# A mixture-of-experts product: gelu half a block later, all splits on VectorE, pairs at another rate, and the scatters of the gate matrix in pairs behind marks

## The chip, the cores and the metric

The kernel runs on one core of one Trainium2 chip. The metric is the device time of the whole program in microseconds (us).

## The reference, cut to what matters

Two transformer blocks are computed for 256 tokens with D = 2048. The change lies in the last part of the second block, a mixture of 16384 experts of which each of 8 heads takes 16 per token:

```python
def peer_ffn(h, w_pq, sub_keys_1, sub_keys_2, w_u, w_v):
    q = (hf @ w_pq).reshape(T, PEER_HEADS, 2, PEER_HALF)
    s1 = jnp.einsum('thd,kd->thk', q[:, :, 0], sub_keys_1).astype(jnp.float32)
    s2 = jnp.einsum('thd,kd->thk', q[:, :, 1], sub_keys_2).astype(jnp.float32)
    v1, i1 = lax.top_k(s1, PEER_TOPK)
    v2, i2 = lax.top_k(s2, PEER_TOPK)
...
    sc, ci = lax.top_k(cand, PEER_TOPK)
...
    experts = e1 * PEER_KEYS + e2
    gates = jax.nn.softmax(sc, axis=-1).astype(h.dtype)
...
        u = jnp.take(w_u, ib, axis=0)
        a = jnp.einsum('td,tkd->tk', hb, u)
        c = gb * jax.nn.gelu(a)
        vv = jnp.take(w_v, ib, axis=0)
        return jnp.einsum('tk,tkd->td', c, vv)
```

## The kernel before, in words

The kernel does not gather rows of w_u per token. It computes the product of all 256 tokens with all 16384 experts, applies gelu, and multiplies by a matrix C that holds each token's gate at its experts and zero elsewhere. C has 128 partitions (the first key, e1) and 128 slices of 257 columns (the second key, e2; 256 tokens and one column of row numbers).

**The u product.** `u_block(e2)` runs for e2 = 0 to 127, in two half blocks b (i = 2 * e2 + b counts half blocks, 0 to 255). A half block has a 512 KB load of w_u into a tile wr (SP's queue, 4 buffers), its rounding to wh on ScalarE (`split_next`, line 1464, 2 buffers), the rest wl = wr - wh on VectorE or POOL (`low`, line 1469, 2 buffers) and 16 matmuls on TensorE (8 of 512 columns and 8 of 256, line 187, into the PSUM tile pp). `split_next(i + 1)` is written ahead of half block i's matmuls. At the end of an e2, line 1502 copies half of pp on ScalarE, 1503 adds the other half on VectorE and 1504 multiplies by a row on POOL (VectorE once all pairs are through). The gelu of that e2 (`tail`, lines 1481 and 1483 on ScalarE) and the product with C (line 1484, POOL, later VectorE) come in the next e2.

**What lies between.** `between` puts other work into each half block, in three phases. First the search for the top 16 (`topk_steps`, lines 1350 to 1420, most of it VectorE's), so many steps per half block as a budget of 18 allows, and then `finish`. In this phase `low` of every second half block is POOL's (line 1466), but for every eighth e2. Then the 128 pairs of tokens, one per half block: `pair_ops` builds one-hot rows (lines 1516 to 1521, VectorE and ScalarE), `pair_mms` multiplies them a half block later into a PSUM tile pq, and after two pairs `quad_end` brings four columns of gates into C (line 1537). Last `places`, which numbers the rows of C that are used by the tokens' first or second half.

**The scatters.** When the places are there, `send(e2)` writes slice e2 of C, 128 rows of 1088 bytes, to rows of a DRAM tensor cd, at the places `posi` (line 1584, an indirect DMA that POOL issues; 124 of them). `u_block`'s loop writes up to 6 of them behind each e2. The order of TensorE, ScalarE and VectorE is as written (`manual_schedule`); POOL's order is left to the scheduler. Behind the u product comes the v product: four slices of C with w_v loaded plainly, then 103 times a load of 128 rows of cd by SP (`fetch`, line 1712), a gather of rows of w_v by POOL (line 1714), their split (lines 1676 and 1683) and the matmuls into py.

Each engine works through its own order and waits at an instruction for semaphores that other engines or DMAs set.

Of the kernel before, what the change touches and what calls it, by code (L numbers as in the profile page):

```python
# [1282 lines left out]
def peer(nc, tc, io, xd, hT, rbc, hp, sp, W, ident, mm, raw_block, split_block, proj_T, blocks, power_rstd, new_pair):  # L1283
    cd = io["cd"]
    with ExitStack() as es:
# [35 lines left out]
        with ExitStack() as pu_stack:  # L1321
# [135 lines left out]
            def split_next(i):  # L1457

                e2, b = divmod(i, 2)
                if e2 == 128:  # L1460
                    return lambda: None
                raw = raw_block(io["w_u"][e2, b])
                hi = W["pool"].tile([128, 1024], F32R, name="wh", bufs=W["hi"])
                nc.scalar.activation(hi, raw, AF.Copy)  # L1464
                eng = nc.gpsimd if b and not topk_done and e2 % 8 else nc.vector

                def low():
                    lo = W["pool"].tile([128, 1024], F32R, name="wl", bufs=W["lo"])
                    eng.tensor_tensor(lo, raw, hi.bitcast(F32), op=OP.subtract)  # L1469
                    parts[i] = hi, lo  # L1470

                return low
# [14 lines left out]
            def u_block(e2):  # L1487
                P = pu.tile([128, 512], F32, name="pp")
                for b in range(2):
                    low = split_next(2 * e2 + b + 1)  # L1490
                    if b == 0:
                        tail()
                    between(low)
                    hi, lo = parts.pop(2 * e2 + b)
                    for j in range(8):
                        k = 8 * b + j
                        mm(P, hi[:, j * 128:(j + 1) * 128], hT[k].rearrange("p s t -> p (s t)"), k == 0, False)
                    for j in range(8):
                        k = 8 * b + j
                        mm(P[:, :256], lo[:, j * 128:(j + 1) * 128], hT[k][:, 0, :], False, k == KT - 1)  # L1500
# [24 lines left out]
            def pair_mms(p, ws):  # L1525
                if p % 2 == 0:
                    bank4[0] = pq.tile([128, 4, 128], F32, name="pq")
                for i, w in enumerate(ws):
                    t = 2 * p + i
                    for a in range(3):  # L1530
                        mm(bank4[0][:, t % 4, :], w[:, 0, :], w[:, 1 + a, :], t % 4 == 0 and a == 0, t % 4 == 3 and a == 2)
                    mm(cnt[:, t // 128, :], w[:, 0, :], w[:, 4, :], t == 0, t == 255)

            def quad_end(q4, n):
                t4 = slice(4 * q4, 4 * q4 + 4)
                v = bank4[0].rearrange("p t e -> p e t")
# [41 lines left out]
            sent = [0]  # L1578

            def send(e2):  # L1580


                src = C.rearrange("p a b -> p (a b)")[:, e2 * 257:e2 * 257 + CROW]
                i = nc.gpsimd.indirect_dma_start(cd, bass.IndirectOffsetOnAxis(posi[:, e2:e2 + 1], 0), src, None).ins  # L1584
# [8 lines left out]
            placing = None  # L1593

            def between(low):


                nonlocal pair, q4, left, topk_done, placing
                if not topk_done or fins:
# [7 lines left out]
                    left += 18  # L1607
# [5 lines left out]
                full = None  # L1613
                if waiting:
                    p, ws = waiting.pop()
                    pair_mms(p, ws)
                    if p % 2:
                        full = p // 2
                if pair < 128:
                    waiting.append((pair, pair_ops(pair)))  # L1620
                    pair += 1
                low()
                if placing and next(placing, "end") == "end":
                    placing = False
                if full is not None:
                    quad_end(full, done[0])
# [5 lines left out]
            pu_stack.enter_context(tc.manual_schedule(engines={mybir.EngineType.PE, mybir.EngineType.Activation, mybir.EngineType.DVE}))  # L1632
            split_next(0)()
            for e2 in range(128):
                u_block(e2)
                if placing is False:
                    for _ in range(6):
                        if sent[0] < min(e2 - 1, NC):
                            send(sent[0])
# [251 lines left out]
```

## Time and profile before

| | |
|---|---|
| median of 3 runs (lowest to highest) | 2949.1 us (2947.26 to 2950.67) |
| the profiled execution's own time | 2950.48 us |
| its span | 2948.7 us |
| mean granted TensorE clock | 0.971 |
| busy: PE, DVE, ACT, POOL | 94%, 64%, 54%, 27% |
| DMA, mean over the span | 191 GB/s |

Times in the profile are us from the span's start. PE is TensorE's matmuls, PEld its loads of weights, DVE is VectorE, ACT ScalarE, POOL GpSimd; SPq is the queue of DMAs that SP issues. L1464 is line 1464 of the kernel before. In a row of the timeline the bracket tells how long the engine was idle before the instruction and what ended that. "issue" means that the profile shows nothing it waited for, "remote" that a semaphore's setter is not shown.

### The profile page before, as it was taken

The page shows a single profiled execution, that of the slowest core. Times are in us where ns is not written, and L with a number is a line of the kernel's source. Part 1 is how long each engine was busy: PE and PEld are TensorE (multiplying, and loading weights), DVE is VectorE, ACT ScalarE, POOL GpSimd, SP SyncE. Part 2 cuts the span into 40 slices and gives each one's busy share as a digit, 9 for nine tenths or more (in the row PEclk, how much of TensorE's full clock was granted, in tenths as well). Part 3 has the DMA queues.
Part 4 walks back from the last instruction along what each step waited for, and adds up shares of the span by engine and source line. Part 5 has one row for each costly group of instructions (what it writes and reads, how often), then busy time and mean ns, then how long its engine had stood idle before and what let it go on. Part 6 is the DMA issues. An engine that isn't in the chain of part 4 may idle for free. (4 is left out here: it accounts for less than half of the span.)

```text
span 2948.7 us, 41341 instructions
## 1 busy us (share of the span) xinstructions
PE 2768.1 (94%) x14566; PEld 2301.3 (78%) x14566; DVE 1898.4 (64%) x3498; ACT 1588.6 (54%) x2951; POOL 798.5 (27%) x703
## 2 busy tenths in 40 slices
PE   8999999999999999999999899999994199999998
PEld 5867788887888888878887678888883087888886
DVE  7545576556766555565657878888882065766665
ACT  4445565445665544444544348888871054655554
POOL 6312320012310000111014442333337622322231
PEclk9999999999999999999999999999997599999999
DMA  6565443654446655666554344444445266988883
GB/s 224 177 223 189 134 139 123 218 187 154 147 144 208 209 183 167 215 211 193 183 179 157 134 157 158 159 158 161 160 144 189 98 216 236 359 298 285 299 308 133
DMA packets 158810, 561.74 MB, mean 191 GB/s; under 512 B 19584, under 2 KB 33536, under 8 KB 145024
## 3 DMA queue, kind: packets, MB, share of 16 engines
q1 hardware_dynamic: 137808, 433.71, 44.9%
q0 software_dynamic: 20784, 125.29, 11.4%
q8 instruction: 117, 1.92, 0.3%
q14 instruction: 101, 0.83, 0.1%
HBM read 531.17 MB, written 27.75 MB: 190 GB/s over the span
## 5 line engine op out<-in xcount | busy, mean ns | idle before, releaser
L204 DVE TENSOR_TENSOR wl<-wr,wh 128x1024 fp32r<-128x1024 f32 (+1 forms) x467 | 600.2, 1287 | 458.9 <-ACT wh L202 385.3
L187 PE MATMUL pp<-hT,wh 128*128 128x512 f32 x2880 | 754.4, 404 | 104.2 <-ACT wh L1464 53.3
L202 ACT ACTIVATE wh<-wr 128x1024 fp32r<-128x1024 f32 (+1 forms) x467 | 492.9, 1056 | 585.0 <-PE pp L187 495.5
L187 PE MATMUL pp<-wh,hT 128*128 128x512 f32 x2688 | 695.6, 399 | 4.6 <-ACT wh L202 2.7
L187 PEld LDWEIGHTS pp<-hT,wh 128*128 128x128 f32 x2880 | 525.0, 192 | 207.3 <-ACT wh L1464 58.8
L187 PEld LDWEIGHTS pp<-wh,hT 128*128 128x128 f32 x2688 | 501.3, 190 | 127.7 <-ACT wh L202 7.8
L187 PEld LDWEIGHTS pp<-hT,wl 128*128 128x128 f32 x2880 | 396.6, 192 | 57.8 <-issue 21.1
L187 PE MATMUL pp<-hT,wl 128*128 128x256 f32 x2880 | 406.6, 284 | 26.2 <-issue 20.3
L187 PE MATMUL pp<-wl,hT 128*128 128x512 f32 x1344 | 374.5, 400 | 12.1 <-DVE wl L204 12.1
L1469 DVE TENSOR_TENSOR wl<-wr,wh 128x1024 fp32r<-128x1024 f32 x230 | 278.7, 1221 | 116.3 <-issue 64.3
L187 PEld LDWEIGHTS pp<-wl,hT 128*128 128x128 f32 x1344 | 248.9, 190 | 70.6 <-DVE wl L204 15.4
L1464 ACT ACTIVATE wh<-wr 128x1024 fp32r<-128x1024 f32 x256 | 268.9, 1050 | 42.1 <-remote 33.1
L1676 ACT ACTIVATE hT<-vb 128x1024 fp32r<-128x1024 f32 x202 | 210.7, 1059 | 131.0 <-PE py L187 100.6
L1683 DVE TENSOR_TENSOR wr<-vb,hT 128x1024 fp32r<-128x1024 f32 x135 | 165.3, 1229 | 76.1 <-PE py L187 55.0
L1714 POOL DMA_INDIRECT vb<-w_v,cb x103 | 128.9, 1252 | 284.1 <-ACT hT L1676 99.7
L1584 POOL DMA_INDIRECT cd<-C,posi x124 | 137.6, 1110 | 138.0 <-DVE C L1484 89.5
L1521 ACT ACTIVATE oh<-oh,gP 128x128 bf16<-128x128 bf16 x512 | 162.0, 389 | 0.0
L187 PE MATMUL py<-hT,c 128*128 128x512 f32 x600 | 152.6, 389 | 0.0
L187 PE MATMUL py<-hT 128*128 128x512 f32 x592 | 150.4, 389 | 0.0
L187 PEld LDWEIGHTS py<-hT,c 128*128 128x128 f32 x600 | 112.6, 188 | 23.4
L187 PEld LDWEIGHTS py<-hT 128*128 128x128 f32 x592 | 111.1, 188 | 23.1
L1683 DVE TENSOR_TENSOR wl<-vb,hT 128x1024 fp32r<-128x1024 f32 x67 | 82.2, 1227 | 34.2 <-PE py L187 27.7
(445 smaller groups left out, 3162.4 us busy)
## 6 DMA issues: line engine op xcount, KB each, us to landing
wr<-w_u SPq DMA_DIRECT2D x256, 512.0 KB
wr<-w_even SPq DMA_DIRECT2D x104, 512.0 KB
wr<-w_out SPq DMA_DIRECT2D x96, 512.0 KB
wr<-w_odd SPq DMA_DIRECT2D x96, 512.0 KB
wr<-w_in SPq DMA_DIRECT2D x64, 512.0 KB
wr<-w_mem SPq DMA_DIRECT2D x32, 512.0 KB
wr<-w_pq SPq DMA_DIRECT2D x32, 512.0 KB
cb<-cd SPq DMA_DIRECT2D x103, 136.0 KB
```

The lines of the kernel that those rows point to most:

```text
L187: nc.tensor.matmul(out, lhsT=lhsT, rhs=rhs, start=start, stop=stop, skip_group_check=True)
L202: nc.scalar.activation(hi, raw, AF.Copy)
L204: (lo_eng or nc.vector).tensor_tensor(lo, raw, hi.bitcast(F32), op=OP.subtract)
L1464: nc.scalar.activation(hi, raw, AF.Copy)
L1469: eng.tensor_tensor(lo, raw, hi.bitcast(F32), op=OP.subtract)
L1521: nc.scalar.activation(w[:, 1 + a, :], w[:, 4, :], AF.Copy, scale=gP[:, a, t:t + 1])
L1584: i = nc.gpsimd.indirect_dma_start(cd, bass.IndirectOffsetOnAxis(posi[:, e2:e2 + 1], 0), src, None).ins
L1676: nc.scalar.activation(hi, src, AF.Copy)
L1683: nc.vector.tensor_tensor(lo, src, hi.bitcast(F32), op=OP.subtract)
L1714: nc.gpsimd.indirect_dma_start(v, None, wide, bass.IndirectOffsetOnAxis(c[:, 256:257].bitcast(I32), 0))
```

## The change

Line numbers shift by a few: 1469, 1484 and 1502 to 1504 are one lower in the changed kernel, and line 1584 is 1586.

- All of `low` is on VectorE.
- `tail` runs in the second half block of an e2 instead of the first, behind the rounding of the next half block.
- The budget for the top-k steps is 14 per half block instead of 18. The last step stands behind half block 76 instead of 59, and the first pair in half block 83 instead of 66.
- The pairs are spread so that they end in half block 194, as before: 94 half blocks have one, 17 have two.
- From half block 197 on, VectorE sets one element of the tile eT behind its `low` (line 1630), and two scatters follow on POOL, each behind a copy of that element (line 1585). 118 of the 124 scatters are sent so, and 6 behind the last `tail`. POOL's order is as written too.

```diff
-                eng = nc.gpsimd if b and not topk_done and e2 % 8 else nc.vector
...
-                    eng.tensor_tensor(lo, raw, hi.bitcast(F32), op=OP.subtract)
+                    nc.vector.tensor_tensor(lo, raw, hi.bitcast(F32), op=OP.subtract)
...
-                    if b == 0:
+                    if b:
                         tail()
-                    between(low)
+                    between(2 * e2 + b, low)
...
+                p = paced[0]
+                nc.gpsimd.tensor_copy(eT[:1, 1, e2:e2 + 1], eT[:1, 0, p:p + 1])
                 i = nc.gpsimd.indirect_dma_start(cd, bass.IndirectOffsetOnAxis(posi[:, e2:e2 + 1], 0), src, None).ins
...
+            q_end = 2 * 97
...
-                    left += 18
+                    left += 14
...
-                if waiting:
-                    p, ws = waiting.pop()
-                    pair_mms(p, ws)
+                full, ws = [], list(waiting)
+                waiting.clear()
+                if pair < 128 and q_from is None:
+                    q_from = i
+                for p, w in ws:
+                    b4 = pair_mms(p, w)
                     if p % 2:
-                        full = p // 2
-                if pair < 128:
+                        full.append((p // 2, b4))
+                while pair < 128 and pair * (q_end - q_from) < 128 * (i + 1 - q_from):
                     waiting.append((pair, pair_ops(pair)))
                     pair += 1
                 low()
+                if placing is False and sent[0] < NC:
+
+                    nc.vector.memset(eT[:1, 0, i:i + 1], 1.0)
+                    paced[0] = i
+                    for _ in range(2):
+                        if sent[0] < min(i // 2 - 1, NC):
+                            send(sent[0])
...
-            pu_stack.enter_context(tc.manual_schedule(engines={mybir.EngineType.PE, mybir.EngineType.Activation, mybir.EngineType.DVE}))
+            pu_stack.enter_context(tc.manual_schedule(engines={mybir.EngineType.PE, mybir.EngineType.Activation, mybir.EngineType.DVE,
+                                                             mybir.EngineType.Pool}))
...
-                if placing is False:
-                    for _ in range(6):
-                        if sent[0] < min(e2 - 1, NC):
-                            send(sent[0])
```

Three places show how the order moves. The first is ScalarE in the top-k phase, two half blocks before the change (junk and rbc are the two buffers that hold an e2's sums):

```order
L1502 ACTIVATE junk<-pp 128x256 [waits PE_49]
L1464 ACTIVATE wh<-wr 128x1024 [waits DMAHW4_49,Activation_49]
L1481 ACTIVATE C<-junk 128x256 [waits Pool_49]
L1464 ACTIVATE wh<-wr 128x1024 [waits DMAHW5_49,DVE_49,PE_49]
L1502 ACTIVATE rbc<-pp 128x256 [waits PE_49]
```

And the same place with the change:

```order
L1501 ACTIVATE rbc<-pp 128x256 [waits PE_49,Activation_49]
L1464 ACTIVATE wh<-wr 128x1024 [waits DMAHW6_49,DVE_49]
L1464 ACTIVATE wh<-wr 128x1024 [waits DMAHW7_49,DVE_49,PE_49]
L1480 ACTIVATE C<-rbc 128x256 [waits Pool_49]
L1501 ACTIVATE junk<-pp 128x256 [waits PE_49,Activation_49]
```

The gelu, which waits for POOL, stood between the two roundings of the weights, and now stands behind both.

The second place is VectorE in the same phase, before (L1350 to L1355 are steps of the top-k, pp is the product):

```order
L1503 TENSOR_TENSOR junk<-junk,pp 128x256 [waits Activation_49]
L1354 MAX C<-C 128x8 [waits DVE_49]
L1355 MAX_INDEX C<-C 128x8 [waits DVE_49]
L1350 MAX C<-C 128x8
L1351 MAX_INDEX C<-C 128x8 [waits DVE_49]
L1352 MATCH_REPLACE C<-C 128x128
L1469 TENSOR_TENSOR wl<-wr,wh 128x1024 [waits DMAHW5_49,PE_49,Activation_49]
```

With the change:

```order
L1502 TENSOR_TENSOR junk<-junk,pp 128x256 [waits Activation_49]
L1468 TENSOR_TENSOR wl<-wr,wh 128x1024 [waits DMAHW4_49,Activation_49]
L1350 MAX C<-C 128x8
L1351 MAX_INDEX C<-C 128x8 [waits DVE_49]
L1352 MATCH_REPLACE C<-C 128x128
L1354 MAX C<-C 128x8 [waits DVE_49]
L1355 MAX_INDEX C<-C 128x8 [waits DVE_49]
L1468 TENSOR_TENSOR wl<-wr,wh 128x1024 [waits DMAHW5_49,PE_49,Activation_49]
```

Every half block's wl is now in VectorE's order, with fewer steps of the top-k between two of them.

The third place is POOL at the first scatters, before:

```order
L1504 TENSOR_TENSOR rbc<-rbc 128x256 [waits DVE_49]
L1484 TENSOR_TENSOR C<-C,rbc 128x252 [waits Activation_49,Pool_49]
L1584 DMA cd<-C,posi 15872x272 [waits DVE_49]
L1584 DMA cd<-C,posi 15872x272 x7
L1584 DMA cd<-C,posi 15872x272 [waits DMASW0_49]
```

With the change:

```order
L1483 TENSOR_TENSOR C<-C,junk 128x252 [waits Activation_49,Pool_49]
L1503 TENSOR_TENSOR rbc<-rbc 128x256 [waits DVE_49]
L1585 COPY eT<-eT 1x1 [waits DVE_49]
L1586 DMA cd<-C,posi 15872x272
L1585 COPY eT<-eT 1x1
L1586 DMA cd<-C,posi 15872x272
L1585 COPY eT<-eT 1x1 [waits DVE_49]
```

Before, a scatter waits for the DMA eight ahead of it at most; now every second one also stands behind a copy that waits for VectorE.

## Rows read from the trace of the kernel before

**Rows 1.** Busy time of each engine, windows from the product's start to the end.

```profile
core 0: us, PE busy (x) PEld busy (x) DVE busy (x) ACT busy (x) POOL busy (x), PEclk, DMA share, GB/s
1536.00:1769.00 233.00, 205.99 (x1119) 176.30 (x1118) 183.01 (x551) 97.35 (x147) 104.82 (x91) 0.96 0.45 149
1769.00:2195.00 426.00, 425.85 (x3075) 376.76 (x3073) 375.18 (x1026) 353.03 (x894) 144.18 (x126) 1.00 0.47 158
...
2210.00:2233.00 23.00, 23.00 (x135) 20.31 (x135) 14.49 (x23) 11.25 (x16) 17.98 (x16) 1.00 0.88 286
2233.00:2363.00 130.00, 26.89 (x97) 21.02 (x96) 11.94 (x16) 8.29 (x12) 86.11 (x88) 0.57 0.35 121
2363.00:2486.00 123.00, 123.00 (x707) 108.25 (x707) 78.98 (x113) 63.30 (x92) 33.54 (x20) 1.00 0.63 211
```

**Rows 2.** What TensorE waited for, 1500 to 2500 us: total, times, longest.

```profile
PE pp L187 <- issue: 63.0, 3, 42.8
```

**Rows 3.** Waits of PE, ACT and DVE, 1536 to 1769 us: total, times, longest.

```profile
PE pp L187 <- ACT wh L1464: 26.5, 23, 3.4
...
ACT C L1481 <- POOL junk L1504: 61.2, 16, 6.3
...
DVE C L1350 <- POOL C L1388: 14.4, 10, 2.9
```

**Rows 4.** Timeline around 1615 us: start, length, instruction, idle time before it.

```profile
1614.36 0.73 POOL L1504 TENSOR_TENSOR rbc<-rbc 128x256 f32<-128x256 f32 x1 [1.96 <-DVE rbc L1503]
...
1615.12 0.42 ACT L1481 ACTIVATE C<-rbc 128x256 f32<-128x256 f32 x1 [5.48 <-POOL rbc L1504]
...
1616.54 2.85 PE L187 MATMUL pp<-hT,wh 128*128 128x512 f32 x7 [2.20 <-ACT wh L1464]
```

**Rows 5.** Line 1469's instructions, 1536 to 1769 us: count, min/median/max ns.

```profile
L1469 DVE TENSOR_TENSOR wl<-wr,wh x40: 1207/1226/1372, 1537.2 to 1767.4; 128x1024 fp32r<-128x1024 f32 x40
L1469 POOL TENSOR_TENSOR wl<-wr,wh x26: 2363/2405/3470, 1544.0 to 1744.6; 128x1024 fp32r<-128x1024 f32 x26
```

**Rows 6.** VectorE's group of line 1503, 1536 to 1769 us: busy, mean ns.

```profile
L1503 DVE TENSOR_TENSOR junk<-junk,pp 128x256 f32<-128x256 f32 x16 | 6.6, 411 | 0.0
```

**Rows 7.** Busy PE, PEld, DVE, ACT on the tile pq, 1536 to 1769 us.

```profile
1536.00:1769.00 233.00, 6.82 (x54) 6.31 (x54) 1.81 (x6) 4.27 (x8) 0.96 0.45 149
```

**Rows 8.** One piece of the stall, all engines (columns as in Rows 1).

```profile
2343.70:2356.50 12.80, 3.78 (x8) 2.48 (x8) 0.00 (x0) 1.14 (x2) 0.00 (x0) 0.50 0.03 11
```

**Rows 9.** Waits of all engines, 2205 to 2365 us.

```profile
ACT junk L1502 <- remote: 66.1, 1, 66.1
```

**Rows 10.** POOL busy with scatters alone (line 1584), clock, DMA, by window.

```profile
2210.00:2233.00 23.00, 17.98 (x16) 1.00 0.88 286
2233.00:2343.70 110.70, 84.41 (x87) 0.57 0.38 133
```

**Rows 11.** Timeline of POOL at three places.

```profile
2231.77 0.96 POOL L1584 DMA_INDIRECT cd<-C,posi  x1 [0.30 <-issue]
...
2371.57 1.69 POOL L1584 DMA_INDIRECT cd<-C,posi  x1 [3.89 <-DVE C L1484]
...
2869.06 1.58 POOL L1714 DMA_INDIRECT vb<-w_v,cb  x1 [4.49 <-ACT hT L1676]
2870.64 0.20 POOL L1749 COPY xg<-vb 128x1 f32<-128x1 f32 x1
2870.99 1.81 POOL L1714 DMA_INDIRECT vb<-w_v,cb  x1 [0.15 <-POOL xg L1749]
```

**Rows 12.** Timeline behind the product's end: SP's loads, first use of a gather.

```profile
2490.49 2.23 SPq L1712 DMA_DIRECT2D cb<-cd  x5
...
2503.11 2.00 ACT L1676 ACTIVATE hT<-vb 128x1024 fp32r<-128x1024 f32 x2 [8.02 <-DMA vb<-w_v,cb]
```

**Rows 13.** Windows around TensorE's idle time behind the product (as Rows 1).

```profile
2500.00:2506.10 6.10, 0.00 (x0) 0.00 (x0) 1.23 (x2) 2.99 (x4) 2.79 (x3) 0.88 1.02 427
2506.10:2520.00 13.90, 13.89 (x50) 11.32 (x51) 10.54 (x11) 8.69 (x11) 2.13 (x2) 0.81 1.02 413
```

More of the change, by code (lines that the diff above doesn't have):

```diff
@@ L1532, in pair_mms, with quad_end @@
                     mm(cnt[:, t // 128, :], w[:, 0, :], w[:, 4, :], t == 0, t == 255)
-            def quad_end(q4, n):
+                return bank4[0]
+            def quad_end(q4, bank, n):
                 t4 = slice(4 * q4, 4 * q4 + 4)
-                v = bank4[0].rearrange("p t e -> p e t")
+                v = bank.rearrange("p t e -> p e t")
                 nc.vector.tensor_tensor(C[:, :n, t4], C[:, :n, t4], v[:, :n], op=OP.mult)
@@ L1576, in places @@
                 nc.vector.tensor_scalar(flag, more[:, 3:4], 0.0, None, op0=OP.is_gt)
-            sent = [0]
+            sent, paced = [0], [0]
             def send(e2):
                 src = C.rearrange("p a b -> p (a b)")[:, e2 * 257:e2 * 257 + CROW]
+                p = paced[0]
+                nc.gpsimd.tensor_copy(eT[:1, 1, e2:e2 + 1], eT[:1, 0, p:p + 1])
                 i = nc.gpsimd.indirect_dma_start(cd, bass.IndirectOffsetOnAxis(posi[:, e2:e2 + 1], 0), src, None).ins
@@ L1592, in peer, with between @@
             pair, waiting = 0, []
-            placing = None
-            def between(low):
-                nonlocal pair, q4, left, topk_done, placing
+            placing = q_from = None
+            q_end = 2 * 97
+            def between(i, low):
+                nonlocal pair, q4, q_from, left, topk_done, placing
                 if not topk_done or fins:
@@ L1612, in between @@
                     return
-                full = None
-                if waiting:
-                    p, ws = waiting.pop()
-                    pair_mms(p, ws)
+                full, ws = [], list(waiting)
[4 more added lines that the diff above has]
+                    b4 = pair_mms(p, w)
                     if p % 2:
-                        full = p // 2
-                if pair < 128:
+                        full.append((p // 2, b4))
+                while pair < 128 and pair * (q_end - q_from) < 128 * (i + 1 - q_from):
                     waiting.append((pair, pair_ops(pair)))
@@ L1622, in between @@
                 low()
+                if placing is False and sent[0] < NC:
[4 more added lines that the diff above has]
+                            send(sent[0])
                 if placing and next(placing, "end") == "end":
                     placing = False
-                if full is not None:
-                    quad_end(full, done[0])
+                for p, b4 in full:
+                    quad_end(p, b4, done[0])
                     q4 += 1
```

## The prediction, made before the changed kernel ran

> **What bounds the kernel now.** I first cut the last part of the span, from the first half block of the u product on, into windows [rows 1]. The reader is to see four different stages. From 2363 to 2486 us TensorE is full: 123.0 us with 707 matmuls. A half block has 16, so 707 are 44.2 half blocks, and one takes 2.79 us when nothing holds it. From 1769 to 2195 TensorE is full as well, 426 us for 128 half blocks, 3.33 us each, since each also carries the matmuls of one pair of tokens (0.54 us). From 1536 to 1769, where VectorE looks for the top 16, TensorE is busy for 206.0 of 233.0 us, and from 2233 to 2363 for only 26.9 of 130.0, at a granted clock of 0.57.
>
> Then I asked what TensorE waited for in these stages [rows 2, 3]. In the late hole the waits have no releaser in the profile ("issue", 63.0 us in 3 waits, the longest 42.8). In the top-k stage 23 waits (26.5 us) ended with ScalarE's wh of line 1464.
>
> The late hole is the larger loss: 97 matmuls are 6 half blocks, worth 16.9 us, so 113 us are lost. It coincides with POOL issuing scatters one behind the other: 16 from 2210 to 2233, where TensorE is still full, and 87 more up to 2343.7 [rows 10], each 0.96 us and 0.30 us of issue apart [rows 11], so 1.27 us. VectorE and ScalarE are busy for 11.9 and 8.3 of the 130 us [rows 1], so none of them is the bound; ScalarE's line 1502, which waits for TensorE's finished product, stands for 66.1 us, released by something remote [rows 9]. And 12.8 us after the last scatter of the burst, with POOL idle and the DMA engines at 0.03, the engines still stand [rows 8]. I read this as the marks that one engine sets for another arriving late while POOL issues scatters at that rate, with a backlog: 103 scatters in 146 us (2210 to 2356.5) is 1.42 us each. The burst is faster than that. Single scatters, one per 5.6 us at 2371 [rows 11], leave TensorE full [rows 1].
>
> **The change, part by part**, against the profiled execution (2950.5 us; its span is 2948.7, and the median of the runs shown, 2949.1, is 1.4 lower).
>
> *Late gelu and lows on VectorE.* In the top-k stage the chain is: POOL's multiply of line 1504 ends at 1615.09, ScalarE's gelu has waited 5.48 us for it, and behind the gelu in ScalarE's order stands the next wh, for which TensorE waits 2.20 us [rows 4]. POOL is late because 26 of the 66 lows are its work, 2.41 us each against 1.23 on VectorE [rows 5]. ScalarE stands 61.2 us for one of the two buffers [rows 3]. The change takes all 26 from POOL and puts the gelu behind the next wh, so both causes go. What becomes late next is VectorE. Its busy time of 183.0 us [rows 1] holds 49.1 of lows (40 x 1.226, rows 5) and 13.1 of line 1503 (two groups of 6.6 [rows 6]); 120.8 remain for the top-k. The budget of 14 for 18 stretches these from 59 half blocks to 76 (by their place in the order). Per half block VectorE then has 120.8/76 = 1.59 + 1.23 + half of 0.41 = 3.02 us, 229.5 us in 76; TensorE has 76 x 2.79 + 6.8 [rows 7] = 218.8. So VectorE is about 10 us behind; I take 10 of loss, with ends of 0 (operations that overlapped POOL's lows get shorter; VectorE's 14.4 us for POOL's copies [rows 3] go too) and 25 (the loss of today, less little).
>
> *Pairs at another rate.* The 128 pairs now lie in 111 half blocks instead of 128, 17 of them with two. TensorE's work is the same. VectorE's 375.2 us in that stage [rows 1] lose 17 lows and half as many adds (24 us), and 351 stand beside 111 x 2.79 + 68.9 = 378.6 on TensorE, 93% instead of 88%. A half block with two pairs costs VectorE 1.23 + 0.21 + 2 x 1.50 = 4.4 us against 3.9 on TensorE; 17 x 0.5 is 9, part of it caught by the two buffers. I take 6, ends 0 and 20.
>
> *Sum of the two.* Before: 659 us for 194 half blocks [rows 1]. The work in them is 194 x 2.79 = 541.3, 6.8 for the top-k and 68.9 for the pairs: 617. So 42 us are lost now and 16 afterwards: **minus 26** (ends: minus 42 and plus 3).
>
> *Paced scatters.* Two per half block, each behind a one-element copy on POOL; the first copy of each two waits for VectorE's memset behind the low. If TensorE's marks come in time, the hole goes: **minus 113**. The wait is put where it can't be in the way for others: what is queued behind it on POOL is only scatters, and VectorE, ScalarE and TensorE wait for none of them in this stage. The 59 memsets lie on VectorE, which has 44 idle us in 123 [rows 1]; if that cover is gone they cost 59 x 0.2 us (the nearest row is POOL's one-element copy [rows 11]) = 12.
>
> *POOL as the new bound.* A scatter takes 0.96 us alone, 1.12 on average (17.98/16) while VectorE works at full rate [rows 10], and up to 1.81 [rows 11]. Copy and gap add 0.20 + 0.15 [rows 11], and a wait for a mark I put at 0.06 per scatter. So 1.53 us each, and 118 of them take 181 us where 59 half blocks take 164.6: POOL ends 16 us behind TensorE. The last 6 scatters come behind that, 9 us. So the rows of C are complete 25 us after the product, plus 2 us to land. Now SP's first load of cb starts at 2490.5 [rows 12], some 4 us behind the product's end at 2486 [rows 1], its first gathered rows are used at 2503.1 [rows 12], and TensorE, out of work from 2500.0 to 2506.1 [rows 13], waits for them. A load later by 25 + 2 - 4 = 23 us moves that by as much: **plus 23**. Ends: plus 6 (scatters of 0.96, POOL keeps up, six remain) and plus 101 (scatters of 1.81: 118 x 2.16 = 255, 90 behind, 13 for the six). I take 1.53 since the 16 scatters of [rows 10] ran beside VectorE's usual work, and the 1.69 and 1.81 of [rows 11] are those that started just as a low or its like began.
>
> *Clock.* Behind today's idle 6.1 us the granted clock is 0.81 for 13.9 us [rows 13], 2.6 us lost. The longer hole will do the same: **plus 3**, ends 0 and 8.
>
> Sum: 2950.5 - 26 - 113 + 23 + 3 = 2837.5, less 1.4 for the median: **2836 us**.
>
> **A rule that speaks against it.** While VectorE works a scatter can take 1.69 us where it takes 0.96 alone [rows 11]. The Trainium skill, page "SBUF — State Buffer", section "Who interferes with whom", says that a VectorE operation of that sort (two SBUF inputs, as the low has) and a POOL operation that reads SBUF exclude each other for a whole instruction, so the scatter's descriptors wait. By that rule each scatter that meets a low is stretched to the low's end; the trace agrees for single cases and shows 1.12 us as the mean.
>
> **Rivals.**
> 1. *Every scatter is stretched.* The mark comes right behind a low, so each pair of scatters starts at the same point of VectorE's order and may always meet the next low or add. Then the upper price holds: plus 101 instead of 23, 2950.5 - 26 - 113 + 101 + 3 - 1.4 = 2914 us. For it: the 1.69 of the spaced scatters, which all start behind the multiply of line 1484. Against it: the mean of 1.12 in 16 scatters.
> 2. *The marks are still late, by half.* Two scatters in 2.79 us are one per 1.40, as fast as the 1.42 that I worked out for the backlog. In the burst each of the 87 scatters past the first 16 cost TensorE 113/87 = 1.30 us. If each of some 100 costs 0.65, that is plus 65; POOL keeps up then (plus 6 for 23): 2950.5 - 26 - 113 + 65 + 6 + 3 - 1.4 = 2884 us. Against a worse run of it: VectorE's mark waits for TensorE's, so POOL is held as soon as the others stand.
> 3. *Slower than before: the stall becomes regular.* If TensorE's mark arrives only when POOL's two scatters are through, the half block and the scatters no longer overlap: 59 x (2 x 1.5 + 2.79) = 342 us for 164.6, plus 177, without the lateness behind it: 2950.5 - 26 - 113 + 177 + 6 + 3 - 1.4 = 2996 us. It decides from 2.4 us of added time per half block on (59 x 2.4 = 140, which uses up 113 + 26). For it: in the burst TensorE got next to nothing done. Against it: from 2210 to 2233 it lost nothing beside 16 scatters at 1.43 us.
> 4. *The pacing doesn't pace.* POOL's own time per scatter is above 1.40, so after a few marks it never waits, and only the copies spread the scatters: 1.53 for 1.27. If what counts is that POOL never rests, the hole stays, shorter by the part in which POOL is held: about 2922 with only the 26 gained. This I count with rival 2.
>
> **How the numbers follow.** About 0.2% (6 us) is what a measurement of this kernel can tell from no change. My forecast (2800 to 2865, with the ends of the small terms) has 0.61. Rival 1 (2865 to 2925) has 0.13, rivals 2 and 4 (2870 to 2925) 0.13, rival 3 and other slow cases 0.10, a time within 0.2% 0.03. Faster: 0.61 + 0.13 + 0.13 = 0.87; same 0.03; slower 0.10. The low end is minus 42, minus 113, plus 6 and no clock loss: 2950.5 - 149 - 1.4 = 2800, with some for a better clock 2798. The high end takes in rivals 1, 2 and 4 up to 2925 and leaves the slower cases out. The likeliest case's own range is 2800 to 2865.
>
> **What would show it.** Right: windows of the stage behind the placing (some 165 us) with TensorE full at a clock of 1.00 and no long "issue" or "remote" waits; scatters at about 1.5 us spacing, the last one some 25 us behind the last matmul into pp, and a hole of about 25 us in front of the first gathered product; in the top-k stage no TensorE waits for wh of over a few us and VectorE busy above 95%. Wrong: scatter durations near 1.8 and a hole of 100 us (rival 1), half blocks of 3.5 to 4 us while scatters run (rival 2), or of over 5 us (rival 3), or a hole of tens of us with waits on "remote" as now (rival 4). A top-k stage that takes 25 us more than its matmuls would make my first term wrong.

## The result, and the profile after

| | before | after |
|---|---|---|
| median (lowest to highest of 4 runs) | 2949.34 us (2947.26 to 2950.67) | 2865.79 us (2864.37 to 2867.30) |
| ratio, 95% interval | | 0.9717 (0.9701 to 0.9734) |
| span of the profiled execution | 2948.7 us | 2865.3 us |
| mean granted clock | 0.971 | 0.986 |

The changed kernel is 83.6 us faster; 113 were forecast (2836 us), with a range of 2798 to 2925 us. The windows of the changed kernel, cut at its own stages (top-k, pairs, scatters beside the u product, the gap behind it, the rest), answer to [rows 1]:

```profile
core 0: us, PE busy (x) PEld busy (x) DVE busy (x) ACT busy (x) POOL busy (x), PEclk, DMA share, GB/s
1537.00:1776.00 239.00, 238.79 (x1385) 209.49 (x1384) 218.97 (x601) 126.45 (x182) 73.56 (x74) 1.00 0.55 183
1776.00:2181.00 405.00, 397.37 (x2824) 340.99 (x2823) 354.05 (x1012) 324.31 (x857) 82.37 (x111) 1.00 0.44 146
2187.00:2352.00 165.00, 165.00 (x948) 145.22 (x948) 109.68 (x216) 80.75 (x121) 147.65 (x174) 1.00 0.87 262
2352.00:2400.50 48.50, 0.39 (x4) 0.19 (x2) 2.85 (x6) 2.11 (x5) 42.72 (x75) 0.56 0.37 134
2400.50:2865.00 464.50, 445.97 (x1932) 367.01 (x1932) 295.13 (x334) 256.88 (x335) 134.15 (x111) 0.98 0.76 278
```

The hole of [rows 1] is gone: from 2187 to 2352 us TensorE is busy for all of the 165.0 us, at a clock of 1.00, while POOL issues scatters. In its place there is a new one of 48.5 us behind the product, in which POOL works for 42.7 us and the other engines for less than 3 each, at a clock of 0.56. The waits of TensorE answer to [rows 2]:

```profile
PE py L187 <- issue: 48.1, 1, 48.1
PE py L187 <- ACT wh L202: 4.9, 2, 2.7
```

The 63.0 us of "issue" in the u product are no longer there, nor the kernel before's waits for ScalarE's wh in it, in the top-k stage and in the hole:

```profile
PE pp L187 <- ACT wh L1464: 53.3, 25, 17.4
```

One wait of 48.1 us stands in front of the v product. Half block starts, taken from TensorE's matmuls, give the bill by stage (a half block's work is 2.79 us, as before):

| stage | before | after | difference |
|---|---|---|---|
| half blocks 0 to 195 (top-k and pairs) | 663.1 | 643.8 | -19.3 |
| 195 to 197 (places) | 8.1 | 6.5 | -1.6 |
| 197 to 255 | 275.4 | 162.0 | -113.4 |
| last half block's end to the span's end | 462.5 | 513.1 | +50.6 |

These sum to -83.7, the spans differ by 83.4.

What the late signals of the kernel before look like, at the beginning of its hole: TensorE's last matmul of an e2 ends at 2236.25 + 1.21 = 2237.46, and ScalarE's copy of the product, which needs nothing else that comes as late, starts at 2244.19, 6.7 us behind it.

```profile
2236.25 1.21 PE L187 MATMUL pp<-hT,wl 128*128 128x256 f32 x8 [1.12 <-issue]
...
2244.19 0.38 ACT L1502 ACTIVATE rbc<-pp 128x256 f32<-128x256 f32 x1 [11.74 <-remote]
```

In the changed kernel, in the middle of the scatters, the same pair is 0.1 us apart (2229.49 to 2229.59):

```profile
2228.38 1.11 PE L187 MATMUL pp<-hT,wl 128*128 128x256 f32 x8
...
2229.59 0.39 ACT L1501 ACTIVATE junk<-pp 128x256 f32<-128x256 f32 x1 [2.39 <-PE pp L187]
```

### The profile page after: what moved, and what is told of

It reads as the page before. It is cut to its first block, busy times and chain, and to the rows that moved or that the text cites. A ratio compares the mean times of both kernels' runs of the same rounds, so it can differ in the third digit from the quotient of the medians.

```text
span 2865.3 us, 41540 instructions
## 1 busy us (share of the span) xinstructions
PE 2759.4 (96%) x14566; PEld 2289.0 (80%) x14566; DVE 1911.6 (67%) x3584; ACT 1583.8 (55%) x2943; POOL 759.0 (26%) x793
## 5 line engine op out<-in xcount | busy, mean ns | idle before, releaser
L187 PE MATMUL pp<-hT,wh 128*128 128x512 f32 x2880 | 735.7, 397 | 0.0
L187 PEld LDWEIGHTS pp<-hT,wh 128*128 128x128 f32 x2880 | 516.3, 189 | 94.3 <-issue 0.3
L187 PE MATMUL pp<-wl,hT 128*128 128x512 f32 x1344 | 374.1, 400 | 10.9 <-DVE wl L204 10.9
L1468 DVE TENSOR_TENSOR wl<-wr,wh 128x1024 fp32r<-128x1024 f32 x256 | 315.3, 1232 | 17.7 <-ACT wh L1464 15.5
L187 PEld LDWEIGHTS py<-hT,c 128*128 128x128 f32 x600 | 112.6, 188 | 23.4
L1586 POOL DMA_INDIRECT cd<-C,posi x124 | 123.8, 999 | 19.4 <-issue 19.4
```

What stands on the lines that cost most here:

```text
L187: nc.tensor.matmul(out, lhsT=lhsT, rhs=rhs, start=start, stop=stop, skip_group_check=True)
L1468: nc.vector.tensor_tensor(lo, raw, hi.bitcast(F32), op=OP.subtract)
```

## The experiments

The first question was which part of the change takes the hole away. Each kernel was timed against the kernel before on the same chip. The sets ran on different chips, so small differences between kernels of two sets are read from the stages too; a stage that no edit touches repeats well (half blocks 0 to 195 take 643.8 us in the changed kernel, 643.5 and 643.6 in two kernels below).

**The copies left out.** The changed kernel with these edits, and POOL's order left to the scheduler as before:

```diff
-                p = paced[0]
-                nc.gpsimd.tensor_copy(eT[:1, 1, e2:e2 + 1], eT[:1, 0, p:p + 1])
...
-                    nc.vector.memset(eT[:1, 0, i:i + 1], 1.0)
-                    paced[0] = i
```

> The changed kernel without the copies in front of the scatters and without VectorE's memsets (POOL's order again left to the scheduler, which puts the scatters one behind the other). Theory A (the scatters' rate makes the hole): scatters 1.27 to 1.45 us apart, the hole of about 113 us returns in the u product, the v product then waits little: 2866 + 113 - 45 = about 2934 us. Rival B (the late gelu and the other order of the first phases did away with the hole, not the copies): TensorE stays full, the scatters end some 36 us earlier than in the changed kernel: about 2830 us.

Measured: 2857.36 us (2856.6 to 2858.95), 8.4 less than the changed kernel; no hole. The window of its scatters, in the columns shown above:

```profile
2191.00:2353.00 162.00, 162.00 (x930) 142.56 (x929) 107.43 (x155) 79.67 (x120) 133.55 (x90) 1.00 0.85 267
```

TensorE is full for 162.0 us and POOL issues 90 scatters in them, one per 1.80 us. Theory A as I had put it falls, since without copies the scatters did not come at 1.27 us; but they did not end 36 us earlier either, as rival B had it (the last starts at 2397.0, 41 us behind the product's end). So the copies are not needed here. What holds the scatters apart instead can be read from the timeline of POOL and VectorE (rows in between left out), which repeats these three scatters:

```profile
2340.57 1.23 DVE L1468 TENSOR_TENSOR wl<-wr,wh 128x1024 fp32r<-128x1024 f32 x1
2340.80 1.82 POOL L1584 DMA_INDIRECT cd<-C,posi  x1 [0.30 <-issue]
2342.42 0.42 DVE L1483 TENSOR_TENSOR C<-C,rbc 128x256 f32<-128x256 f32 x1 [0.63 <-ACT wh L1464]
2342.77 1.22 DVE L1468 TENSOR_TENSOR wl<-wr,wh 128x1024 fp32r<-128x1024 f32 x1
2342.93 1.89 POOL L1584 DMA_INDIRECT cd<-C,posi  x1 [0.31 <-issue]
2345.12 0.96 POOL L1584 DMA_INDIRECT cd<-C,posi  x1 [0.30 <-issue]
```

Two of three scatters take nearly twice the 0.96 us of the third; 1.82, 1.89 and 0.96 with their gaps of 0.30 make 5.6 us, two half blocks of TensorE. The two long ones start during a low of VectorE and end 0.8 us behind that low's end (2341.80 and 2343.99), so POOL runs in step with VectorE's work.

**Copies without marks.** The copies read one element that is always there:

```diff
-                nc.gpsimd.tensor_copy(eT[:1, 1, e2:e2 + 1], eT[:1, 0, p:p + 1])
+                nc.gpsimd.tensor_copy(eT[:1, 1, e2:e2 + 1], eT[:1, 0, 0:1])
...
-                    nc.vector.memset(eT[:1, 0, i:i + 1], 1.0)
-                    paced[0] = i
```

> The changed kernel with every copy reading one element that is always there, and without VectorE's memsets: copies stay, no scatter waits for a mark. Theory A (it is the time that the copies take, since POOL waited for a mark only once in the changed kernel): the same time within 3 us, 2866. Rival C (the marks hold POOL back so that TensorE's signals arrive): a hole of tens of us returns, 2890 or more.

Measured: 2870.81 us (2869.61 to 2871.58). It is 5 us slower, but no hole of late signals came back: TensorE is full until two half blocks before the product's end, and then waits once,

```profile
PE pp L187 <- ACT c L1658: 51.2, 1, 51.2
```

for ScalarE's rounding of the first slice of C for the v product, which here stands ahead of the last wh in ScalarE's order and starts as soon as POOL's last copy has ended, at 2394.90 (the next run tells why):

```profile
2394.72 0.18 POOL L1584 COPY eT<-eT 1x1 f32<-1x1 f32 x1
2394.93 0.42 ACT L1658 ACTIVATE c<-C 128x256 fp32r<-128x256 f32 x1 [53.97 <-issue]
```

So the marks do nothing against the hole, as the changed kernel's own trace says: POOL waited for a mark once, 13.2 us before the first copy, and never again.

**Tiles of their own for marks and copies.**

```diff
+        mark = pk.tile([1, 60], BF, name="mark")
+        took = pk.tile([1, 96], BF, name="took")
...
-                nc.gpsimd.tensor_copy(eT[:1, 1, e2:e2 + 1], eT[:1, 0, p:p + 1])
+                nc.gpsimd.tensor_copy(took[:, e2 % 96:e2 % 96 + 1], mark[:, p:p + 1])
```

> The changed kernel with the marks and the copies in two small tiles of their own instead of eT. Theory D (the 48 us without work behind the u product come about because c2 of the first slices takes eT's place and so waits for the last copy, line 1661): ScalarE's line 1661 and TensorE's products from w_v go on at once, the hole splits: about 20 us of products first, then 25 to 30 us of waiting for the gathers; the time falls by 3 to 20 us, to 2846 to 2863. Rival E (the products wait for the scatters or their queue): the hole of 48 us stays as it is, 2866.

Measured: 2850.77 us (2850.15 to 2851.62), 15.0 less. Theory D holds. In the changed kernel the chain at the end of the gap can be read off the timeline: the last copy (of eT) ends at 2400.01, ScalarE's line 1661 starts at 2400.03, TensorE at 2400.50, and SP's first load of cb only at 2403.33.

```profile
2399.83 0.18 POOL L1585 COPY eT<-eT 1x1 f32<-1x1 f32 x1
2400.03 0.42 ACT L1661 ACTIVATE c<-C 128x256 fp32r<-128x256 f32 x1 [44.04 <-issue]
...
2400.50 3.78 PE L187 MATMUL py<-wh,c 128*128 128x512 f32 x8 [48.11 <-issue]
2403.33 1.41 SPq L1721 DMA_DIRECT2D cb<-cd  x1
```

Line 1661 writes the tile c2, and `c_place` gives the first slice eT's memory; the copies read and write eT, so the tile is free only behind the last of them. With tiles of their own TensorE goes on at once, for 16.5 us, and then waits 39.9 us. The wh that ends this wait belongs to the last slice with w_v loaded plainly, but stands in ScalarE's order behind line 1663 on the first rows of C read back (cb), which waited 43.28 us for their load, that is for the end of the scatters:

```profile
PE py L187 <- ACT wh L202: 39.9, 1, 39.9
2406.89 0.89 ACT L1663 ACTIVATE c<-cb 128x256 fp32r<-128x256 f32 x2 [43.28 <-DMA cb<-cd]
```

**A memset on POOL in place of the copies.** No marks; the memset reads no SBUF:

```diff
-                nc.gpsimd.tensor_copy(took[:, e2 % 96:e2 % 96 + 1], mark[:, p:p + 1])
+                nc.gpsimd.memset(took[:, e2:e2 + 1], 1.0)
```

> The changed kernel with a one-element memset on POOL, in a tile of its own, in place of each copy, and no marks: the instruction reads no SBUF. If the copies' 0.7 us come from VectorE's lows holding them up while they read, the memset takes about 0.2 us and the scatters stand 1.35 to 1.5 us apart. Theory A with a threshold near 1.42 us per scatter: the hole comes back in part, 2830 to 2900 us. Rival F (any other instruction of POOL between two scatters is enough): TensorE stays full, the scatters end 30 us earlier: about 2825 us.

Measured: 2855.54 us (2854.44 to 2856.67), no hole. The memset takes 0.09 us and the gap is 0.31 in all, as without anything between. But the scatters did not get closer, since what a copy had waited now falls on the scatter behind it:

```profile
2340.41 0.09 POOL L1585 MEMSET took<- 1x1 bf16 x1
2340.72 1.88 POOL L1586 DMA_INDIRECT cd<-C,posi  x1 [0.21 <-issue]
2342.60 0.09 POOL L1585 MEMSET took<- 1x1 bf16 x1
2342.91 0.96 POOL L1586 DMA_INDIRECT cd<-C,posi  x1 [0.21 <-issue]
```

Here 1.88 and 0.96 us, where the changed kernel has 0.98 for nearly every scatter and 0.18 to 1.17 for the copies. POOL is held up by VectorE, whichever of its instructions comes at that moment. Rival F foresaw the absence of the hole, but not the time; theory A with its threshold was not put to the test, because the distance was 1.60 us for the first 16 scatters and 1.83 after that.

So with the late gelu neither copies nor marks nor an instruction between was needed. What was left is the gelu and the other phases. The next three kernels separate them.

**Early gelu with the copies.** The changed kernel with one edit:

```diff
-                    if b:
+                    if b == 0:
                         tail()
```

> The changed kernel with the gelu back in the first half block of the next e2 (copies, marks and everything else of the change stay). Theory G (the hole needs the early gelu: ScalarE's next wh stands behind a chain TensorE, ScalarE, VectorE, VectorE, ScalarE that late signals stretch past a half block; once TensorE stops, w_u's loads and VectorE's lows stop too and nothing slows the scatters): a hole of tens of us returns although the copies are there, 2890 to 2950 us. Rival H (what keeps TensorE full is the copies or the order in which the scatters are issued): no hole, 2866 us within some us.

Measured: 2877.49 us (2876.26 to 2878.30), no hole: TensorE takes 162.0 us from half block 197 to 255, as with the late gelu. Theory G, that the early gelu is enough for the hole, falls. POOL waited for a mark once, 12.0 us before the first copy, so it is the copies that count here. The first 85 scatters stand 158/85 = 1.86 us apart:

```profile
2203.00:2361.00 158.00, 106.92 (x85) 1.00 0.81 264
```

The top-k stage is longer by 16 us (254.8 us for 83 half blocks, 239.0 with the late gelu), the pair stage shorter by 4.

**Early gelu without the copies.** The same edit in the kernel without copies:

> The run without copies (2857 us), with the gelu back in the first half block. Theory G: the hole returns, about 2857 + 113 - 40 = 2930 us, and as in the kernel before the time varies from run to run by tens of us. Rival H': the hole was done away with by the other order of the phases or the place at which the scatters are issued: 2857 us. If this run has the hole and the one with copies has not, the copies protect as well.

Measured: 2943.63 us (2939.58 to 2945.99). The hole is back, with all its size: 275.1 us from half block 197 to 255. The first row is up to its beginning, the second the hole (POOL's scatters alone):

```profile
2202.00:2225.00 23.00, 17.90 (x16) 1.00 0.84 287
2225.00:2353.00 128.00, 85.89 (x89) 0.56 0.35 121
```

16 scatters in 23 us, as in [rows 10], then 89 in 128.

**The kernel before with the late gelu alone.** One edit in the kernel before: `if b == 0` becomes `if b` at the call of `tail`.

> The kernel before with one edit: the gelu in the second half block. Theory G: no hole in the u product; the scatters then run beside a full TensorE at 1.66 us each and end some 45 us behind it, so 2949 - 113 + 40 = about 2876 us, less what the top-k stage gains (0 to 20). Rival H: the hole stays, 2930 to 2950.

Measured: 2862.94 us (2862.03 to 2864.87). This line alone gives 85.6 us, as much as the whole change. Its scatters run beside a full TensorE (columns as above) at 160.5/89 = 1.80 us each:

```profile
2192.00:2354.00 162.00, 162.00 (x930) 142.57 (x930) 107.44 (x154) 79.68 (x120) 133.67 (x89) 1.00 0.85 266
```
The scatters alone (line 1584), from the first on:

```profile
2193.50:2354.00 160.50, 133.67 (x89) 1.00 0.85 266
```

With early gelu the copies take the hole away, with late gelu nothing more is needed. Both make the scatters stand 1.8 us and more apart. That gave **theory R**: the hole depends on the distance of the scatters, and the late gelu works by VectorE's order. With the early gelu VectorE runs the lows of both half blocks one behind the other (2.35 us, then a pause), and 4 of the first 16 scatters of the kernel before are stretched (over 1.2 us); with the late gelu the product with C (line 1483 in the rows of the kernel without copies above) stands between them, and there 54 of the first 88 are. VectorE in the kernel before:

```profile
2212.88 0.43 DVE L1484 TENSOR_TENSOR C<-C,rbc 128x256 f32<-128x256 f32 x1 [0.48 <-ACT rbc L1483]
2213.22 2.35 DVE L1469 TENSOR_TENSOR wl<-wr,wh 128x1024 fp32r<-128x1024 f32 x2
2216.99 0.42 DVE L1503 TENSOR_TENSOR junk<-junk,pp 128x256 f32<-128x256 f32 x1 [1.42 <-ACT junk L1502]
```

The rival is that ScalarE's order, with more slack for late signals, is what counts. Three runs put this to the test.

**Early gelu with the memset**, which is an instruction between the scatters and takes 0.09 us (the edit of the early gelu in the kernel with the memset):

> Early gelu as in the two runs with it, and a one-element memset on POOL before each scatter, no copies and no marks. With the late gelu this memset took 0.09 us and left the distance of two scatters as it is without anything between (0.31 us of gap for 0.30). Theory R (the hole depends on the distance of the scatters, which the order of VectorE's lows sets to 1.43 us with the early gelu and 1.58 and more with the late one, and the copies to 1.70): the hole returns, 2930 to 2950 us. Rival I (any instruction of POOL between two scatters keeps the signals going): no hole, about 2870 us.

Measured: 2945.67 us (2940.05 to 2947.97). The hole is back, at 1.44 us. An instruction between is not what counts; this is what theory R foresaw.

**A copy before every second scatter, early gelu:**

```diff
-                nc.gpsimd.memset(took[:, e2:e2 + 1], 1.0)
+                if e2 % 2:
+                    nc.gpsimd.memset(took[:, e2:e2 + 1], 1.0)
+                else:
+                    nc.gpsimd.tensor_copy(took[:, e2:e2 + 1], oneb[:1])
```

> As the run with the memset and the early gelu, with a one-element copy instead of the memset before every second scatter, so a distance between 1.43 and 1.71 us, about 1.55. Theory R with its limit between 1.43 and 1.58: no hole, the scatters end earlier than with a copy before each (2877), about 2860 to 2875 us; if the limit is above 1.55, the hole returns, over 2910.

Measured: 2935.95 us (2918.12 to 2942.34). At 1.55 us the hole is back, though it begins a little later (half block 208 instead of 206). So the limit lies above 1.55: most of the stretch that I had given it, 1.43 to 1.58, falls away, and the forecast of no hole with it.

**Late gelu, with VectorE's lows together.** ScalarE's order is the late one; VectorE's product with C goes behind the second low while the scatters run:

```diff
-                    if b:
-                        tail()
+                    mult = tail() if b else None
                     between(2 * e2 + b, low)
+                    if mult:
+                        mult()
```

(`tail` returns the product with C as a function where all pairs are through.)

> The late gelu with the memset in place of the copies (2855.5 us, no hole, scatters at 1.66 us), where VectorE's product with C stands behind the second low instead of between the two while the scatters run. ScalarE's order stays the late one. Theory R: the scatters come as close as with the early gelu (about 1.43 us at first) and the hole returns, 2900 to 2950 us. Theory G (the slack of the late gelu on ScalarE is what counts): no hole, the scatters end up to 25 us earlier, 2830 to 2856 us.

Measured: 2904.30 us (2890.71 to 2909.96), 49 more than the same kernel with VectorE's other order. The scatters stand 1.43 us apart again, and the late signals are back, with the late gelu. ScalarE's copy of a product that TensorE finished at 2206.51 + 1.21 = 2207.72 starts at 2209.84, released by "remote":

```profile
2206.51 1.21 PE L187 MATMUL pp<-hT,wl 128*128 128x256 f32 x8 [0.98 <-issue]
...
2209.84 0.38 ACT L1509 ACTIVATE rbc<-pp 128x256 f32<-128x256 f32 x1 [6.17 <-remote]
```

So the late gelu works on the hole through VectorE's order. That order is not enough for the hole by itself, since the early gelu with copies has the lows together as well, and no hole: the distance counts. The hole is smaller than with the early gelu (251.0 us for the 58 half blocks, 275.7 there); that ScalarE's slack takes off this part is a guess, which no run shows.

Ten kernels side by side, in the order of their distances. The distance is the start of the 17th scatter less that of the first, by 16, and then that of the 11th to the 81st by 70:

| kernel | gelu | between scatters | first 16, us | 11th to 81st, us | half blocks 197 to 255, us | time, us |
|---|---|---|---|---|---|---|
| before | early | nothing | 1.43 | 1.28 | 275.4 | 2949.3 |
| early gelu, no copies | early | nothing | 1.43 | 1.28 | 275.1 | 2943.6 |
| early gelu, memset | early | memset | 1.44 | 1.40 | 275.7 | 2945.7 |
| late gelu, lows together | late | memset | 1.44 | 1.44 | 251.0 | 2904.3 |
| early gelu, every second | early | copy, memset | 1.55 | 1.39 | 265.6 | 2936.0 |
| no copies | late | nothing | 1.60 | 1.83 | 162.0 | 2857.4 |
| memset | late | memset | 1.60 | 1.83 | 162.0 | 2855.5 |
| before, late gelu | late | nothing | 1.73 | 1.84 | 162.0 | 2862.9 |
| changed | late | copy | 1.89 | 1.87 | 162.0 | 2865.8 |
| early gelu, copies | early | copy | 1.90 | 1.87 | 162.0 | 2877.5 |

Neither the gelu's place nor what stands between the scatters sorts the kernels with the hole from those without it; the distance does. In the kernels with the hole the second column of distances is a consequence as well, since VectorE stands for most of that time. The four kernels that are not in the table have 1.87 to 1.89 and 1.87 us, and no late signals.

The load of the DMA engines does not sort the kernels. These are the 23 us from the first scatter on (columns as in [rows 1]), of the kernel with a copy before every second scatter, where the hole follows, and of the one with the late gelu and the memset, where none does:

```profile
2204.00:2227.00 23.00, 23.00 (x136) 20.32 (x135) 15.45 (x23) 11.26 (x16) 20.41 (x29) 1.00 0.87 274
2190.00:2213.00 23.00, 23.00 (x133) 20.20 (x133) 16.01 (x25) 10.81 (x16) 19.83 (x29) 1.00 0.89 277
```

One thing is left open: wherever the scatters stand far enough apart, it is VectorE that holds up a scatter or a copy. No run spaced them by a pause of another kind.

**Ten slices taken plainly.** A try at a better version: with tiles of their own, 40 us are still spent on waiting for the scatters' end. So 10 instead of 4 slices of C go with all rows of w_v loaded, which needs no gather:

```diff
-ND = 4
+ND = 10
-FIRST = (0, 76)
-SECOND = (26, 103)
+FIRST = (0, 72)
+SECOND = (25, 98)
```

> The run with marks and copies in tiles of their own (2851 us) with 10 instead of 4 slices of C taken plainly with all of their w_v, so 118 scatters, and bounds of the packed rows that fit (98 gathers instead of 103). If the 40 us without work behind the u product are only the wait for the scatters' end, 6 more slices fill 33 us of it, the scatters end 10 us earlier, and TensorE saves about 16 us of packed products: 2851 - 40 + 33 - 16 = about 2828 us. If the gathers wait for something else, the hole stays: 2860 or more.

Measured: 2842.18 us (2841.36 to 2842.74), 8.6 less than with four, where 23 were expected, and 3.6% below the kernel before. The wait fell from 39.9 to 10.9 us:

```profile
PE py L187 <- ACT hT L1663: 10.9, 1, 10.9
```

The terms expected were 40 us less of waiting and 17 more of products (33 less 16); the wait fell by 29.0 and the rest grew by about 20. A wait remains because the scatters, though 6 fewer, ended no earlier (the last starts at 2401.2, 2402.0 with four). Behind the u product a scatter and its copy took (34.46 + 9.30)/31 = 1.41 us of POOL here and (36.31 + 7.50)/37 = 1.18 with four slices; VectorE splits more of w_v in that time, which fits the delay seen above.

**A larger top-k budget.** In that kernel `left += 14` becomes `left += 15`:

> The run with ten slices taken plainly (2842 us) with a top-k budget of 15 instead of 14 per half block, so that the pairs start 6 half blocks earlier and 11 instead of 17 half blocks have two. In the changed kernel the pair stage takes 23 us more than its matmuls, 1.4 us for each half block with two pairs, and the top-k stage loses nothing, with VectorE busy for 93% of it. If the loss is that of the half blocks with two pairs and VectorE has the room, 6 x 1.4 = 8 us go: 2834 us. If VectorE becomes the bound of the top-k stage, the time stays at 2842 or rises.

Measured: 2842.49 us (2840.77 to 2844.18), the same. The pair stage loses 18.7 us instead of 23.4 (416.8 us for 118 half blocks, whose work is 398.1), but the top-k stage now loses 4.5 (226.1 for 221.6). What is won on one side of the border is lost on the other. That VectorE is the bound on both sides is likely, not shown: it is busy for 92% of the time ahead of the border and for 87% behind it.

## Why the prediction was right, and where it was off

The time (2866) lies in the range, 30 us above the forecast of 2836 and just above the 2800 to 2865 of the likeliest case. By stages, the front part gained 20.9 us where 26 were foreseen, the scatter stage 113.4 where 113 were, and the end lost 50.6 where 26 were. By the prediction's own steps:

- *Paced scatters, minus 113.* The size is right: 113.4 us. The reason given for it, that copies and marks spread the scatters, is half right: the copies are enough (early gelu with copies: no hole), the marks do nothing, and the copies are not needed here, since with the late gelu alone the scatters already stand 1.8 us apart. The term is the whole of the hole, so whatever takes the hole away gives the same number, and the number does not speak for the reason. I had read from [rows 8, 9, 10] that signals come late when scatters come too fast, and that reading holds; the rate of the backlog that I read with it, 1.42 us, is no limit, since the hole is there at 1.55 as well. What I missed is that the late gelu is itself a part that changes the rate, since it moves VectorE's lows apart. I had cost it in the top-k stage only.
- *POOL as the new bound, plus 23.* This is the step that failed in size: the end is 50.6 us later, 26 with the clock's 3 were foreseen. Of the 24.6 us between them, 15.0 come from the copies' tile (below), and the rest from the term that was mis-sized, the 1.53 us per scatter. From the first scatter to the product's end they stood 1.86 us apart. The scatters alone (line 1586, POOL busy, clock, DMA share, GB/s), beside the product and behind it:

```profile
2187.00:2352.00 165.00, 87.16 (x87) 1.00 0.87 262
2352.00:2402.00 50.00, 36.66 (x38) 0.56 0.37 135
```
And the copies alone (line 1585), in the same windows:

```profile
2187.00:2352.00 165.00, 60.51 (x87) 1.00 0.87 262
2352.00:2402.00 50.00, 6.70 (x37) 0.56 0.37 135
```

  A scatter took 87.16/87 = 1.00 us, as little as could be hoped, but a copy 60.51/87 = 0.70, where I had put the 0.20 of a single row [rows 11]; behind the product it is 6.70/37 = 0.18. I took the mean of 1.12 for scatters from a stretch with VectorE's old order, and let the copies go free. So 37 scatters were left at the product's end, and POOL ended 49 us behind it instead of 25. One row was misread on the way: the 1.81 of [rows 11] is a gather's (line 1714), not a scatter's, and a longer scatter stood among the 16:

```profile
2214.44 1.96 POOL L1584 DMA_INDIRECT cd<-C,posi  x1 [0.30 <-issue]
```
- *Clock, plus 3.* The kernel before already pays 2.6 us behind its own gap [rows 13], so only what goes beyond that is a loss. By these two windows the changed kernel loses about 4 us (5.50 x 0.44 + 11.12 x 0.12 = 3.8), some 1 us more:

```profile
2400.50:2406.00 5.50, 5.50 (x14) 4.34 (x15) 0.41 (x1) 0.13 (x1) 0.82 (x2) 0.56 0.42 122
2416.00:2430.00 14.00, 11.12 (x41) 8.69 (x42) 8.36 (x9) 8.42 (x11) 1.72 (x1) 0.88 1.03 425
```

- *The rule that speaks against it.* The Trainium skill, page "SBUF — State Buffer", section "Who interferes with whom", by which a VectorE operation with two SBUF inputs and a POOL operation that reads SBUF shut each other out, fits the traces better than the sum did: a copy takes up to 1.17 us while VectorE works and 0.18 when it stands, a scatter 1.82 to 1.89 and 0.96. The section itself infers that a VectorE operation of this kind leaves POOL's writing of descriptors alone; these scatters were stretched all the same, and the measurement decides. It says that only a POOL operation that reads SBUF is held up by such a VectorE operation, and the memset, which reads none, took 0.09 us throughout. Rival 1 put 2.16 us on each scatter throughout; the 1.86 lies in the middle, because copy and scatter share one delay.
- *What I did not see at all* is that the copies hold the tile eT, whose memory the v product's first slice takes. This cost 15.0 us.
- *Top-k stage:* 10 us of loss foreseen, none measured (239.0 us for 238.4 of work). VectorE's busy time stayed at 219.0 of 239; some of its operations got shorter than I let them (the eight of line 1417 took 1.73 us each before and 0.82 after), now that POOL has no lows in that stage.
- *Pair stage:* 6 us of loss foreseen, 23.4 measured (404.8 us for 381.4), beyond the end of 20. About 19 of them are there with the early gelu too. The 17 half blocks with two pairs take 4.24 us on average where their matmuls are 3.87, and the ones behind them 3.6 for 3.33: that is some 11 us. The rest lies in half blocks with one pair, and its cause stays open; the budget of 15, with 11 such half blocks, gave back 4.7 us of the 8 expected.
- *The rivals.* Rival 4's first half is what happened: POOL never waited for a mark after the first. Its second half (the hole stays) did not. Rivals 2 and 3 did not show in the changed kernel. Rival 2's doubt, that 1.40 us is too close, was justified: the early gelu with scatters at 1.43 us pays the full price.

## What to carry to other kernels

Where engines stand on signals that come late, count how closely POOL issues its indirect DMAs in that stretch, and ask what sets that distance; an edit on another engine can change it, as the late gelu did through VectorE's order. Pacing by a mark does nothing when the paced engine is the slower one: look whether the wait ever ends last. An instruction put in for its timing alone also holds the memory that it touches; give it a tile that nothing else wants.

## What the runs showed of the hardware

- With scatters of 128 rows of 1088 bytes from POOL at 1.55 us or less apart (five kernels), signals between the engines came late, by 2 to 7 us at first and by tens of us later (half block 208 of the kernel before took 67.4 us), and the 58 half blocks of that stretch took 89 to 114 us more; at 1.60 for the first 16 and 1.83 after that, or more (five kernels), they came in time, with DMA engines busier (0.81 to 0.87, against 0.35 in the hole of the kernel before). The limit lies between, if the mean distance is the right measure, and which path the signals share with the scatters was not found.
- The hole may keep itself alive: while it lasts VectorE does little (11.9 of 130 us [rows 1]), and the scatters of the kernel before go at 1.27 us. No run tests this.
- The size of the hole varies: on one chip the kernel before ran from 2906 to 2949 us in 7 runs, while no kernel without it spread over more than 4 us.
- A one-element copy on POOL takes 0.18 us when VectorE stands and 0.70 on average while it works; a memset of one element takes 0.09 in both cases.
